# Indirect transfers that leave out empty slots, accumulating transfers that add the experts' results, and 32 unused bytes in SBUF

## The chip, the core and the metric

The program runs on one core of a Trainium2 chip: TensorE (PE) multiplies, VectorE (DVE) and ScalarE (ACT) work on tiles in SBUF and PSUM, GpSimd (POOL) does a little arithmetic and issues the indirect transfers, SyncE (SP) issues the other transfers, and 16 DMA engines carry all of them. The metric is the device time of one execution in microseconds. The kernel before took 2285.03 us (median of three runs, 2282.73 to 2285.18).

## The reference, cut to what matters

Two transformer blocks run over 256 tokens of width 1024, all in fp32. Most of the time goes into the mixture of experts of the first block's second layer: each token goes to its two best experts of eight, and an expert is a SwiGLU of width 3584.

```python
def moe_swiglu(xn, router, w_gu, w_down):
    logits = (xn @ router).astype(jnp.float32)
    top_v, top_i = lax.top_k(logits, TOP_K)              # TOP_K = 2 of N_EXPERTS = 8
    w = jax.nn.softmax(top_v, axis=-1)
    comb = jnp.sum(jax.nn.one_hot(top_i, N_EXPERTS, dtype=jnp.float32) * w[..., None], axis=-2)
    out = jnp.zeros_like(xn)
    for e in range(N_EXPERTS):
        out = out + comb[..., e:e + 1] * swiglu(xn, w_gu[e], w_down[e])
    return out
```

256 tokens times two choices over eight experts is 64 tokens for an expert on average.

## The kernel before

**Weights.** Every weight streams once from HBM. `fetch` (L473) loads 1 MB, four blocks of 128x512 fp32, into one of four `raw` buffers; ACT rounds it to `wh` (fp32r), DVE takes the rest `wl = raw - wh` (`split`, L395 and L396, 128x1024 at a time), and PE multiplies three times for each block: xh by wh, xl by wh, xh by wl. So 1 MB gives two `wh`, two `wl` and, in the experts, twelve matmuls of 512 columns. A `raw` buffer is free again, and SP can issue the next load, when DVE has made its second `wl`.

**Experts.** An expert has 128 slots, its tokens stand in the first of them, and the others are empty. For each expert (`expert`) there are seven blocks j: 48 matmuls with `moe_gu` weights, the activation (`ff_s`), and four transposes `tr<-cst,ff_s` that turn the result for the second product. Then come two halves n of the second product: 2 x 84 matmuls with `moe_down`. A branch serves experts with more than 128 tokens; the trace has no instruction of it.

**Rows in and out.** `mo_rows` in HBM holds the tokens' rows. For experts 1 to 7 `slots` (L1245) gathers 128 rows of 4 KB into `mo_got` by an indirect transfer with a list of row numbers `mo_ix`; an empty slot reads row 0. For experts 0 to 6 the result `mo_y` goes out by one indirect transfer for each half n (L1295) to `mo_res` in HBM: 512 rows for the tokens' first and second choice, and 128 spare rows for the empty slots, so that each slot writes a row of its own. `slot_tables` computes the row numbers on DVE with small operations on one to nine columns. Expert 7 goes another way: its result is brought back to the tokens by a matmul with `mo_PT` and added into `res` by DVE (L1305).

**Collecting.** During expert 7, at blocks j = 2 and 3, `collect` loads `mo_res` back (L1326, two transfers of 512 KB for each half n, on SP's queue between the weights), and POOL adds them into the residual tiles `res` (L1329, eight additions of 128x512).

**Order.** The instructions of each engine stand in one fixed order, which a scheduler made from the program; each engine runs its own list in order and waits on semaphores. A wait at the head of a list holds everything behind it. Tiles come from stocks (`sm`, `part`, `wp`) that lie behind the constant tiles (`keep`) in SBUF.

Of the kernel before, what the change touches and what calls it, by code (L numbers as in the profile page):

```python
# [7 lines left out]
F32 = mybir.dt.float32  # L8
F32R = mybir.dt.float32r
I32 = mybir.dt.int32  # L10
U32 = mybir.dt.uint32
AF = mybir.ActivationFunctionType
ALU = mybir.AluOpType
# [3 lines left out]
S = 256  # L17
D = 1024
NE = 8
# [4 lines left out]
TAPS_PE = 20  # L24
POOL_WINDOWS = (2, 4, 8, 16)
HQ = 64

# [65 lines left out]
def prep(i):  # L93

    f = {k: np.asarray(v) for k, v in i.items()}
    a = {}
# [6 lines left out]
    w = f["ev_w_in"][0].reshape(D, 4, 4, 128).transpose(0, 2, 1, 3).reshape(D, 2048)  # L103
# [13 lines left out]
    w = f["od_dw_w"][0][:TAPS_PE].reshape(TAPS_PE // 4, 4, 8, 4, 32).transpose(4, 2, 1, 0, 3)  # L117
# [12 lines left out]
    r = lambda s, n: list(range(s, s + n))  # L130
# [11 lines left out]
    w = f["w_o_2"].reshape(2, 5, 256, D)[:, [3, 4, 0, 1, 2]].reshape(2, 1280, D)  # L142
# [49 lines left out]
    w = Rows()  # L192
# [7 lines left out]
        w.add(f"lam{l}", f["diff_lambda_2"][l])  # L200
    a["rows"] = w.array().reshape(2, 1, -1)
    a["token"] = np.arange(S, dtype=np.float32).reshape(2, 128).T.copy()
    slot = 2 * S + np.arange(128, dtype=np.float32)
    a["spare"] = np.stack([slot, -slot], axis=1)
    a["bigrows"] = np.ascontiguousarray(np.stack([f["final_norm"], f["od_norm_moe"][0], f["od_pw2_b"][0]]))

    p = np.arange(128)
    t = np.arange(S)
    rc = []
    for win in POOL_WINDOWS:  # L210
        left = win // 2
        right = win - 1 - left
        n = np.minimum(t + right, S - 1) + 1 - np.maximum(t - left, 0)
# [90 lines left out]
class Build:  # L304
# [315 lines left out]
    def setup(self):  # L620
        nc, A = self.nc, self.A
        self.res = [self.keep(D, f"res{b}") for b in range(2)]
        cst = self.keep(384, "cst")
        ncol = A["cols"].shape[1]
        self.cols = self.keep(ncol, "cols")
        nc.scalar.dma_start(cst[:, :128], A["consts"][:, :128])
        nc.scalar.dma_start(self.cols[:, :8], A["cols"][:, :8])
        x = lambda n: [nc.sync.dma_start(self.res[b][:, n * 512:n * 512 + 512], A["x"][:, b, n * 512:n * 512 + 512]) for b in range(2)]
        x(0)
        self.ahead("w_in0", whole=False)  # L630
        x(1)
# [12 lines left out]
        self.warm(6)  # L644
        self.nrow = A["rows"].shape[2]
        self.rows, self.pre2, self.mem2 = {}, {}, {}
# [567 lines left out]
    def slot_tables(self, e):  # L1214

        nc = self.nc
        v = nc.vector
        P = self.picked  # L1220
        cws, rws, cw = self.slot_factors(e, P, self.moe_state[2])
        if e < NE - 1:
            to = self.sm(1, "mo_to")
            f = self.sm(NE + 1, "mo_to")
            v.tensor_copy(f, cw[:, NE + 2:])
            v.scalar_tensor_tensor(to, f[:, :1], self.spare[:, 1:2], f[:, 1 + e:2 + e], ALU.mult, ALU.add)
            back = self.sm(1, "mo_tx", I32)
            v.tensor_tensor(back, to, self.spare[:, 0:1], ALU.add)
        else:
            tr = self.scp(256)  # L1230
            for b in range(2):
                self.tp(tr[:, b * 128:b * 128 + 128], P[:, b])
            back = self.keep(S, "mo_PT", F32R)
            nc.scalar.copy(back, tr)
        return back, cws, rws, cw[:, NE + 1:NE + 2]

    def slots(self, e):


        nc = self.nc  # L1240
        back, cws, rws, at = self.slot_tables(e)
        ix = self.sm(1, "mo_ix", I32)
        nc.vector.tensor_copy(ix, at)
        got = self.sm(D, "mo_got")
        nc.gpsimd.indirect_dma_start(got, None, self.moe_state[1], bass.IndirectOffsetOnAxis(ap=ix.bitcast(U32), axis=0))  # L1245
        return got, back, cws, rws

    def turn(self, slots):
# [11 lines left out]
    def expert(self, e, rest, then=None):  # L1260

        nc = self.nc
        v = nc.vector
        gh, gl, back, cws, rws = self.turn(self.next_slots) if e else self.gathered
        xh = lambda k, b: gh[:, k]
        xl = lambda k, b: gl[:, k]
        hh = self.feat("mhh", F32R, 4, (8, 128))
        hl = self.feat("mhl", F32R, 4, (8, 128))
        base = e * D * 2 * DFE
        for j in range(7):  # L1270
            next(rest, None)
            pg, = self.ts(xh, xl, "moe_gu", base + 2 * j * D * 512, 8, nb=1)
            if e < NE - 1 and j == 2:
                self.pick(e + 1)
            if e < NE - 1 and j == 4:
                self.next_slots = self.slots(e + 1)
            if e == NE - 1 and j in (2, 3):
                self.collect(j - 2)
            pu, = self.ts(xh, xl, "moe_gu", base + (2 * j + 1) * D * 512, 8, nb=1)
            s = self.sm(512, "ff_s")  # L1280
            nc.scalar.activation(s, pg, AF.Silu, scale=rws)
            v.scalar_tensor_tensor(s, pu, rws, s, ALU.mult, ALU.mult)  # L1282
            tr = self.trp(4, 128)
            for k in range(4):
                self.tp(tr[:, k], s[:, k * 128:k * 128 + 128])
            self.split(hh[4 * j:4 * j + 4], hl[4 * j:4 * j + 4], tr)
        xh = lambda k, b: hh[k]
        xl = lambda k, b: hl[k]
        base = e * DFE * D
        for n in range(2):  # L1290
            py, = self.ts(xh, xl, "moe_down", base + n * DFE * 512, DFE // 128, nb=1)
            if not then:
                y = self.sm(512, "mo_y")
                nc.scalar.activation(y, py, AF.Copy, scale=cws)
                nc.gpsimd.indirect_dma_start(self.results[n], bass.IndirectOffsetOnAxis(ap=back.bitcast(U32), axis=0), y, None)  # L1295
                continue
            yh = self.sm(512, "mo_yh", F32R)
            yl = self.sm(512, "mo_yl", F32R)
            self.split_gain(yh, yl, py, cws)
            for b in range(2):  # L1300
                po = self.scp(512)
                self.mm(po, back[:, b * 128:b * 128 + 128], yh, True, False)
                self.mm(po, back[:, b * 128:b * 128 + 128], yl, False, True)
                r = self.res[b][:, n * 512:n * 512 + 512]
                v.tensor_tensor(r, po, r, ALU.add)  # L1305
            then.half(n)

    def clear_results(self):


        nc = self.nc
        zero = self.sm(512, "mo_zero")
        nc.gpsimd.memset(zero, 0.0)
        self.results = [self.dram.tile([2 * S + 128, 512], F32, name=f"mo_res{n}") for n in range(2)]
        for y in self.results:
            nc.scalar.dma_start(y[:2 * S].rearrange("(a p) d -> p a d", p=128), zero.unsqueeze(1).to_broadcast([128, 4, 512]))

        self.spare = self.keep(2, "mo_sp")
        nc.sync.dma_start(self.spare, self.A["spare"])

    def collect(self, n):

        nc = self.nc
        for w in range(2):
            z = self.sm((2, 512), "mo_z")
            nc.sync.dma_start(z, self.results[n][w * S:w * S + S].rearrange("(b p) d -> p b d", p=128))  # L1326
            for b in range(2):
                r = self.res[b][:, n * 512:n * 512 + 512]
                nc.gpsimd.tensor_tensor(r, r, z[:, b], ALU.add)  # L1329


    def angles(self):
# [767 lines left out]
```

## Time and profile before

| | us |
|---|---|
| median of three runs | 2285.03 |
| the profiled execution | 2284.27 |
| its span, first to last instruction | 2282.4 |
| PE busy | 2252.5 |
| DVE busy | 1798.6 |
| ACT busy | 1444.3 |
| POOL busy | 115.1 |

The profiled execution is 1.9 us longer than its span, and 0.76 us below the median of the runs. PE counts as busy in nearly all of the span, but its matmuls overlap and their ends are modelled, so how full PE really is has to be read from the time between matmuls in a stretch without a wait, not from the share. The granted clock was 0.999 of full on average.

### The profile page before, as it was taken

What the parts mean: (1) busy time and instruction counts of PE and PEld (TensorE: products, weight loads), DVE (VectorE), ACT (ScalarE), POOL (GpSimd) and SP (SyncE); (2) the same over time, 40 slices, a digit from 0 to 9 for tenths busy, and PEclk for the clock granted to TensorE, in tenths of its full rate; (3) what the DMA queues carried; (4) which work ended last, traced back from release to release, by engine and by line L of the source; (5) the groups of instructions that cost most, each with busy time, mean ns of one, the idle gap of its engine ahead of it and who ended that gap; (6) DMA issues with size and microseconds to landing.
All of it is one profiled execution on the core that took longest, in us unless ns stands there. A gap on an engine that the chain in (4) does not pass through costs nothing.

```text
span 2282.4 us, 34629 instructions
## 1 busy us (share of the span) xinstructions
PE 2252.5 (99%) x13069; PEld 1935.2 (85%) x13069; DVE 1798.6 (79%) x2601; ACT 1444.3 (63%) x2005; POOL 115.1 (5%) x163
## 2 busy tenths in 40 slices
PE   8999999999999999999999999989999999999999
PEld 8999998888878788888788878867788998888997
DVE  7656656986698898889898989888877885876883
ACT  5555545466567777777777777767765544665542
POOL 2100001301000000000000000020000000000000
PEclk9999999999999999999999999999999999999999
DMA  7544755954599989999999999989623555513553
GB/s 280 194 152 166 252 192 203 265 186 162 184 365 354 379 346 368 360 388 360 388 368 381 362 376 366 378 345 346 226 74 119 197 190 177 181 56 131 199 179 120
DMA packets 90891, 588.63 MB, mean 258 GB/s; under 512 B 11232, under 2 KB 12512, under 8 KB 24032
## 3 DMA queue, kind: packets, MB, share of 16 engines
q1 hardware_dynamic: 84752, 570.20, 67.7%
q0 software_dynamic: 4048, 12.97, 1.9%
q10 hardware_dynamic: 1920, 3.22, 0.4%
q8 instruction: 103, 1.69, 0.3%
q14 instruction: 68, 0.56, 0.1%
HBM read 577.31 MB, written 9.04 MB: 257 GB/s over the span
## 4 chain that ended last, share of the span: by engine, by line
PE 64%; DMA 4%; DVE 3%; ACT 1%; issue 1%; POOL 0%; ACTq 0%; DVEq 0%; POOLq 0%
PE acc L372 59%; DMA raw<-in_moe_gu_dram 3%; PE tr L376 3%; DVE wl L396 2%; PE sc L372 2%; ACT wh L395 1%; DMA raw<-in_moe_down_dram 0%; DMA ahead<-in_moe_gu_dram 0%; PE tr L372 0%; DVE res L556 0%; DVE xl L400 0%; POOL res L2043 0%; ACT at_p L1805 0%; DVE ff_s L1282 0%; DVE at_nm L1801 0%
## 5 line engine op out<-in xcount | busy, mean ns | idle before, releaser
L396 DVE TENSOR_TENSOR wl<-raw,wh 128x1024 fp32r<-128x1024 f32 x1054 | 1258.0, 1227 | 305.1 <-PE acc L372 176.9
L395 ACT CAST wh<-raw 128x1024 fp32r<-128x1024 f32 x1054 | 1060.1, 1047 | 431.5 <-PE acc L372 342.0
L372 PE MATMUL acc<-wh,mo_g 128*128 128x512 f32 x1568 | 488.8, 393 | 2.4 <-ACT wh L395 2.4
L372 PE MATMUL acc<-xl,wh 128*128 128x256 f32 x1440 | 399.1, 277 | 3.3 <-DVE xl L400 3.3
L372 PE MATMUL acc<-xh,wh 128*128 128x256 f32 x1440 | 399.7, 279 | 0.9 <-ACT xh L399 0.8
L372 PE MATMUL acc<-xh,wl 128*128 128x256 f32 x1440 | 398.0, 277 | 0.4 <-DVE wl L396 0.4
L372 PEld LDWEIGHTS acc<-wh,mo_g 128*128 128x128 f32 x1568 | 295.3, 189 | 64.8 <-ACT wh L395 3.5
L372 PE MATMUL acc<-wl,mo_g 128*128 128x512 f32 x784 | 314.8, 401 | 5.4 <-DVE wl L396 5.2
L372 PEld LDWEIGHTS acc<-xl,wh 128*128 128x128 f32 x1440 | 270.5, 188 | 5.2 <-DVE xl L400 4.5
L372 PEld LDWEIGHTS acc<-xh,wh 128*128 128x128 f32 x1440 | 270.0, 188 | 2.0 <-ACT xh L399 1.7
L372 PEld LDWEIGHTS acc<-xh,wl 128*128 128x128 f32 x1440 | 270.6, 188 | 0.6 <-DVE wl L396 0.6
L372 PEld LDWEIGHTS acc<-wl,mo_g 128*128 128x128 f32 x784 | 147.6, 188 | 49.4 <-DVE wl L396 21.4
L372 PE MATMUL acc<-wl,mhh 128*128 128x512 f32 x448 | 178.7, 399 | 2.4 <-DVE wl L396 1.6
L372 PE MATMUL acc<-wh,mhl 128*128 128x512 f32 x448 | 176.1, 393 | 0.0
L372 PE MATMUL acc<-wh,mhh 128*128 128x512 f32 x448 | 175.3, 391 | 0.0
L372 PEld LDWEIGHTS acc<-wl,mhh 128*128 128x128 f32 x448 | 84.2, 188 | 25.5 <-DVE wl L396 8.7
L372 PE MATMUL acc<-wl,hh 128*128 128x512 f32 x264 | 104.0, 394 | 0.0
L372 PE MATMUL acc<-wh,hl 128*128 128x512 f32 x264 | 103.5, 392 | 0.0
L372 PE MATMUL acc<-wh,hh 128*128 128x512 f32 x264 | 102.8, 390 | 0.0
L372 PEld LDWEIGHTS acc<-wh,mhl 128*128 128x128 f32 x448 | 84.1, 188 | 18.4
L372 PEld LDWEIGHTS acc<-wh,mhh 128*128 128x128 f32 x448 | 84.3, 188 | 17.2
L395 ACT CAST mhh<-tr 128x512 fp32r<-128x512 f32 x56 | 32.9, 588 | 94.8 <-PE tr L376 94.8
(439 smaller groups left out, 3103.8 us busy)
## 6 DMA issues: line engine op xcount, KB each, us to landing
raw<-in_moe_gu_dram SPq DMA_DIRECT2D x222, 1024.0 KB, 7.0
raw<-in_moe_down_dram SPq DMA_DIRECT2D x112, 1024.0 KB, 6.1
raw<-in_gu_dram SPq DMA_DIRECT2D x66, 1024.0 KB, 4.9
raw<-in_down_dram SPq DMA_DIRECT2D x30, 1024.0 KB, 4.8
raw<-in_w_in_b_dram SPq DMA_DIRECT2D x20, 1024.0 KB, 5.0
raw<-in_wkv_dram SPq DMA_DIRECT2D x16, 1024.0 KB, 5.0
raw<-in_pw_dram SPq DMA_DIRECT2D x12, 1024.0 KB, 4.8
raw<-in_wq_dram SPq DMA_DIRECT2D x8, 1024.0 KB, 4.8
```

What stands on the lines that cost most here:

```text
L372: self.nc.tensor.matmul(out, lhsT=l, rhs=r, start=start, stop=stop)
L376: self.nc.tensor.transpose(out, in_, self.ident[:n, :n])
L395: self.nc.scalar.copy(h, src)
L396: self.nc.vector.tensor_tensor(l, src, h.bitcast(F32), ALU.subtract)
```

## The change

Three edits. The indirect transfers get a bound: `bounds_check` with `oob_is_err=False` leaves out a row whose number lies past the bound. `slot_tables` now makes both lists of row numbers at once (`mo_tx`, two columns), and an empty slot gets 4096 (`PAST`), which is past either bound; so gathers for experts 1 to 6 read, and scatters for experts 0 to 6 write, the filled slots alone. For expert 7 the list is a plain copy, and an empty slot still reads row 0. The spare rows of `mo_res` and the small table `mo_sp` go.

`collect` becomes eight transfers on POOL's queue, each of which adds 128 rows of 2 KB from `mo_res` to a piece of `res` in SBUF (`accum_op`). They stand at block j = 0 of expert 7 for both halves, and the loads `mo_z` and POOL's eight additions go.

`self.keep(8, "shift")` takes 32 bytes of each partition behind `res`. `mo_sp`, which goes, took two numbers of the same pool.

```diff
     def setup(self):
         self.res = [self.keep(D, f"res{b}") for b in range(2)]
+        self.keep(8, "shift")
...
         cws, rws, cw = self.slot_factors(e, P, self.moe_state[2])
+        f = self.sm(NE + 2, "mo_f")
+        v.tensor_copy(f, cw[:, NE + 1:])
         if e < NE - 1:
-            to = self.sm(1, "mo_to")
-            f = self.sm(NE + 1, "mo_to")
-            v.tensor_copy(f, cw[:, NE + 2:])
-            v.scalar_tensor_tensor(to, f[:, :1], self.spare[:, 1:2], f[:, 1 + e:2 + e], ALU.mult, ALU.add)
-            back = self.sm(1, "mo_tx", I32)
-            v.tensor_tensor(back, to, self.spare[:, 0:1], ALU.add)
...
+            to = self.sm(2, "mo_to")
+            v.scalar_tensor_tensor(to, f[:, 1:2].to_broadcast([128, 2]), -PAST, f[:, 0:3 + e:2 + e], ALU.mult, ALU.add)
+            ix = self.sm(2, "mo_tx", I32)
+            v.tensor_scalar(ix, to, PAST, None, ALU.add)
+            return ix[:, 1:2], cws, rws, ix[:, 0:1]
...
-        ix = self.sm(1, "mo_ix", I32)
-        nc.vector.tensor_copy(ix, at)
         got = self.sm(D, "mo_got")
-        nc.gpsimd.indirect_dma_start(got, None, self.moe_state[1], bass.IndirectOffsetOnAxis(ap=ix.bitcast(U32), axis=0))
+        nc.gpsimd.indirect_dma_start(got, None, self.moe_state[1], bass.IndirectOffsetOnAxis(ap=ix.bitcast(U32), axis=0),
+                                     bounds_check=S - 1, oob_is_err=False)
...
-            if e == NE - 1 and j in (2, 3):
-                self.collect(j - 2)
+            if e == NE - 1 and j == 0:
+                self.collect()
...
-                nc.gpsimd.indirect_dma_start(self.results[n], bass.IndirectOffsetOnAxis(ap=back.bitcast(U32), axis=0), y, None)
+                nc.gpsimd.indirect_dma_start(self.results[n], bass.IndirectOffsetOnAxis(ap=back.bitcast(U32), axis=0), y, None,
+                                             bounds_check=2 * S - 1, oob_is_err=False)
...
-    def collect(self, n):
-
-        nc = self.nc
-        for w in range(2):
-            z = self.sm((2, 512), "mo_z")
-            nc.sync.dma_start(z, self.results[n][w * S:w * S + S].rearrange("(b p) d -> p b d", p=128))
-            for b in range(2):
-                r = self.res[b][:, n * 512:n * 512 + 512]
-                nc.gpsimd.tensor_tensor(r, r, z[:, b], ALU.add)
+    def collect(self):
+
+        for n in range(2):
+            for w in range(2):
+                for b in range(2):
+                    r = self.res[b][:, n * 512:n * 512 + 512]
+                    row = (2 * w + b) * 128
+                    self.nc.gpsimd.dma_start(r, self.results[n][row:row + 128], accum_op=ALU.add)
```

On POOL's list at the end of the experts, before (`mo_res_2946` is half 0 of the results, `mo_res_2947` half 1, `res_69` and `res_70` the residual's two pieces):

```order
L1245 DMA mo_got<-mo_rows,mo_ix 128x1024
L1295 DMA mo_res_2946<-mo_y,mo_tx 640x512
L1295 DMA mo_res_2947<-mo_y,mo_tx 640x512
L1329 TENSOR_TENSOR res_69<-res_69,mo_z 128x512
L1329 TENSOR_TENSOR res_70<-res_70,mo_z 128x512
```

There are eight such additions, four for each half. The same place now (`mo_res_2947` is half 0, `mo_res_2948` half 1):

```order
L1245 DMA mo_got<-mo_rows,mo_tx 128x1024
L1296 DMA mo_res_2947<-mo_y,mo_tx 512x512
L1327 DMA res_69<-mo_res_2947 128x512
L1327 DMA res_70<-mo_res_2947 128x512
L1327 DMA res_69<-mo_res_2947 128x512
L1327 DMA res_70<-mo_res_2947 128x512
L1296 DMA mo_res_2948<-mo_y,mo_tx 512x512
L1327 DMA res_69<-mo_res_2948 128x512
```

The four accumulating transfers of half 0 stand ahead of expert 6's last scatter, and those of half 1 behind it. On SP's list, before, the loads of the results stand among expert 7's weights:

```order
L473 DMA raw<-in_moe_gu_dram 128x2048 x11
L1326 DMA mo_z<-mo_res_2946 128x2x512 x2
L473 DMA raw<-in_moe_gu_dram 128x2048 x5
L1326 DMA mo_z<-mo_res_2947 128x2x512 x2
L473 DMA raw<-in_moe_gu_dram 128x2048 x12
```

Now nothing stands between them:

```order
L472 DMA raw<-in_moe_gu_dram 128x2048 x28
L472 DMA raw<-in_moe_down_dram 128x2048 x8
L2025 DMA brow<-in_bigrows_dram 128x1024
```

The lists of PE and ACT differ in a few places only, where a small group moved by a few instructions; DVE's has five instructions fewer.

## Rows read from the trace of the kernel before

**Rows 1.** The page, parts 1 and 2: engines, and DMA share in 40 slices.
```profile
PE 2252.5 (99%) x13069; PEld 1935.2 (85%) x13069; DVE 1798.6 (79%) x2601; ACT 1444.3 (63%) x2005; POOL 115.1 (5%) x163
DMA  7544755954599989999999999989623555513553
```

**Rows 2.** Stretches of the last experts (first row: columns).
```profile
core 0: us, PE busy (x) PEld busy (x) DVE busy (x) ACT busy (x) POOL busy (x), PEclk, DMA share, GB/s
1448.00:1488.00 40.00, 39.87 (x176) 32.19 (x175) 34.11 (x31) 30.53 (x34) 1.95 (x2) 1.00 1.00 398
1488.00:1528.00 40.00, 34.16 (x139) 25.25 (x139) 35.08 (x30) 26.14 (x30) 15.00 (x8) 0.96 0.88 339
```

**Rows 3.** The chain that ended last, 1483 to 1564 (start us, us, what).
```profile
1483.88 0.44 PE tr L376 x4
...
1493.66 9.43 DMA raw<-in_moe_gu_dram
...
1503.60 2.32 DVE wl L396
...
1551.11 0.44 PE tr L376 x4
1551.54 11.07 PE acc L372 x48
1562.61 0.44 PE tr L376 x4
```

**Rows 4.** DVE in order of time, 1494 to 1525 (start us, us, what).
```profile
1497.41 4.03 DVE L396 TENSOR_TENSOR wl<-raw,wh 128x1024 fp32r<-128x1024 f32 x2 [0.25 <-ACT wh L395]
1501.77 6.41 DVE L396 TENSOR_TENSOR wl<-raw,wh 128x1024 fp32r<-128x1024 f32 x4 [0.33 <-ACT wh L395]
...
1508.77 2.35 DVE L396 TENSOR_TENSOR wl<-raw,wh 128x1024 fp32r<-128x1024 f32 x2
...
1514.78 4.23 DVE L396 TENSOR_TENSOR wl<-raw,wh 128x1024 fp32r<-128x1024 f32 x2 [0.71 <-ACT wh L395]
```

**Rows 5.** POOL in order of time, 1440 to 1530.
```profile
1451.62 0.98 POOL L1295 DMA_INDIRECT mo_res<-mo_y,mo_tx  x1 [100.21 <-ACT mo_y L1294]
1470.89 0.97 POOL L1295 DMA_INDIRECT mo_res<-mo_y,mo_tx  x1 [18.28 <-ACT mo_y L1294]
1496.83 8.00 POOL L1329 TENSOR_TENSOR res<-res,mo_z 128x512 f32<-128x512 f32 x4 [24.97 <-DMA mo_z<-mo_res]
1514.39 7.00 POOL L1329 TENSOR_TENSOR res<-res,mo_z 128x512 f32<-128x512 f32 x4 [9.56 <-DMA mo_z<-mo_res]
```

**Rows 6.** Transfers issued 1486 to 1520 (xcount, KB each, median us to landing).
```profile
raw<-in_moe_gu_dram SPq DMA_DIRECT2D x10, 1024.0 KB, 9.0
mo_z<-mo_res SPq DMA_DIRECT2D x4, 512.0 KB, 8.4
```

**Rows 7.** POOL's queue of transfers, whole span (packets, MB, share of 16 engines).
```profile
q0 software_dynamic: 4048, 12.97, 1.9%
```

**Rows 8.** The same queue, 620 to 1610, and its issues.
```profile
q0 software_dynamic: 2128, 7.34, 1.9%
...
mo_res<-mo_y,mo_tx POOLq DMA_INDIRECT x14, 6.9
mo_got<-mo_rows,mo_ix POOLq DMA_INDIRECT x7, 9.9
```

**Rows 9.** POOL in order of time, 720 to 760.
```profile
725.33 1.02 POOL L1295 DMA_INDIRECT mo_res<-mo_y,mo_tx  x1 [58.08 <-ACT mo_y L1294]
744.59 0.97 POOL L1295 DMA_INDIRECT mo_res<-mo_y,mo_tx  x1 [18.24 <-ACT mo_y L1294]
745.87 1.49 POOL L1245 DMA_INDIRECT mo_got<-mo_rows,mo_ix  x1 [0.30 <-issue]
```

**Rows 10.** The chain, 745 to 1160.
```profile
749.94 9.97 DMA raw<-in_moe_gu_dram
```

**Rows 11.** Tile res, 1480 to 1640 (ns min/median/max, first and last start).
```profile
L1305 DVE TENSOR_TENSOR res<-sc,res x4: 680/686/693, 1582.8 to 1607.5; 128x512 f32<-128x512 f32 x4
```

**Rows 12.** Tiles mo_ix and mo_sp.
```profile
L1243 DVE CAST mo_ix<-sc x7: 152/154/158, 663.0 to 689.6; 128x1 int32<-128x1 f32 x7
L1319 SPq DMA_DIRECT2D mo_sp<-in_spare_dram x1: 425/425/425, 38.8 to 38.8; - x1
```

**Rows 13.** What PE waited for, 1610 to the end (us, times, longest).
```profile
PE tr L376 <- DVE at_o L1845: 1.2, 2, 0.7
```

More of the change, by code (lines that the diff above doesn't have):

```diff
@@ L26 @@
 HQ = 64
+PAST = 4096.0
 def _inv_freq(rot):
@@ L202, in prep @@
     a["token"] = np.arange(S, dtype=np.float32).reshape(2, 128).T.copy()
-    slot = 2 * S + np.arange(128, dtype=np.float32)
-    a["spare"] = np.stack([slot, -slot], axis=1)
     a["bigrows"] = np.ascontiguousarray(np.stack([f["final_norm"], f["od_norm_moe"][0], f["od_pw2_b"][0]]))
@@ L1221, in slot_tables @@
         cws, rws, cw = self.slot_factors(e, P, self.moe_state[2])
+        f = self.sm(NE + 2, "mo_f")
+        v.tensor_copy(f, cw[:, NE + 1:])
         if e < NE - 1:
-            to = self.sm(1, "mo_to")
-            f = self.sm(NE + 1, "mo_to")
-            v.tensor_copy(f, cw[:, NE + 2:])
-            v.scalar_tensor_tensor(to, f[:, :1], self.spare[:, 1:2], f[:, 1 + e:2 + e], ALU.mult, ALU.add)
-            back = self.sm(1, "mo_tx", I32)
-            v.tensor_tensor(back, to, self.spare[:, 0:1], ALU.add)
-        else:
-            tr = self.scp(256)
-            for b in range(2):
[L1232 to L1235, printed above, removed]
+            to = self.sm(2, "mo_to")
[3 more added lines that the diff above has]
+            return ix[:, 1:2], cws, rws, ix[:, 0:1]
+        tr = self.scp(256)
+        for b in range(2):
+            self.tp(tr[:, b * 128:b * 128 + 128], P[:, b])
+        back = self.keep(S, "mo_PT", F32R)
+        nc.scalar.copy(back, tr)
+        ix = self.sm(1, "mo_tx", I32)
+        v.tensor_copy(ix, f[:, 0:1])
+        return back, cws, rws, ix
     def slots(self, e):
         nc = self.nc
-        back, cws, rws, at = self.slot_tables(e)
-        ix = self.sm(1, "mo_ix", I32)
-        nc.vector.tensor_copy(ix, at)
+        back, cws, rws, ix = self.slot_tables(e)
         got = self.sm(D, "mo_got")
-        nc.gpsimd.indirect_dma_start(got, None, self.moe_state[1], bass.IndirectOffsetOnAxis(ap=ix.bitcast(U32), axis=0))
+        nc.gpsimd.indirect_dma_start(got, None, self.moe_state[1], bass.IndirectOffsetOnAxis(ap=ix.bitcast(U32), axis=0),
+                                     bounds_check=S - 1, oob_is_err=False)
         return got, back, cws, rws
@@ L1313, in clear_results @@
         nc.gpsimd.memset(zero, 0.0)
-        self.results = [self.dram.tile([2 * S + 128, 512], F32, name=f"mo_res{n}") for n in range(2)]
+        self.results = [self.dram.tile([2 * S, 512], F32, name=f"mo_res{n}") for n in range(2)]
         for y in self.results:
-            nc.scalar.dma_start(y[:2 * S].rearrange("(a p) d -> p a d", p=128), zero.unsqueeze(1).to_broadcast([128, 4, 512]))
-        self.spare = self.keep(2, "mo_sp")
-        nc.sync.dma_start(self.spare, self.A["spare"])
-    def collect(self, n):
-        nc = self.nc
-        for w in range(2):
-            z = self.sm((2, 512), "mo_z")
-            nc.sync.dma_start(z, self.results[n][w * S:w * S + S].rearrange("(b p) d -> p b d", p=128))
-            for b in range(2):
-                r = self.res[b][:, n * 512:n * 512 + 512]
-                nc.gpsimd.tensor_tensor(r, r, z[:, b], ALU.add)
+            nc.scalar.dma_start(y.rearrange("(a p) d -> p a d", p=128), zero.unsqueeze(1).to_broadcast([128, 4, 512]))
+    def collect(self):
+        for n in range(2):
+            for w in range(2):
+                for b in range(2):
+                    r = self.res[b][:, n * 512:n * 512 + 512]
+                    row = (2 * w + b) * 128
+                    self.nc.gpsimd.dma_start(r, self.results[n][row:row + 128], accum_op=ALU.add)
     def angles(self):
```

## The prediction, written before the changed kernel ran

> **What bounds the kernel now.** I read the engines' busy times first: PE is busy for 2252.5 us of the span, and the DMA engines are at nine tenths through the slices of the experts and near half elsewhere [rows 1]. A share alone does not say which of the two sets the end, so I went to the chain that ended last. Between two waits it is a regular beat: 48 matmuls in 11.07 us and four transposes in 0.44, so that one group of transposes follows the last by 11.50 us (1551.11 to 1562.61) [rows 3]. That is PE at its own pace, 0.23 us for a matmul of 512 columns. A block of that length uses 16 weight tiles of 128x512 fp32, 4.19 MB, which asks for 365 GB/s. Then I cut the last experts into stretches: from 1448 to 1488 the DMA engines had no idle share at all and moved 398 GB/s [rows 2]. So in the experts PE is the bound and DMA stands some 8% behind it: whatever holds PE is paid in full, and transfers that are added or left out count as far as they exceed this margin.
>
> [...]
>
> **The change part by part.** *The additions on POOL and the loads mo_z go.* From the transposes at 1483.88 to those at 1562.61 there are six beats (expert 7's blocks 1 to 6): 78.73 us where six undisturbed ones take 6 x 11.50 = 69.0 [rows 3]. The stretch loses 9.7 us. DVE's own excess is 1.68 + 1.71 + 1.88 = 5.3 us [rows 4]; the rest is what stands in order behind it, the loads of mo_z beside the weights (median landing 9.0 us here, and one of 9.43 on the chain [rows 3, 6]), and the lower clock of the stretch. All of it hangs on these additions and loads, and both leave the place: -9.7 us. What is late next there is PE itself.
>
> *Eight accumulating transfers come.* They move what mo_z moved, 2.1 MB, but on POOL's queue and earlier: the order puts the first four right behind expert 6's scatter of half 0, issued at 1451.62, and the last four behind that of half 1 at 1470.89 [rows 5]. Each group waits for the scatter to land (median 6.9 us [rows 8]), and in a group the third transfer adds to the same bytes as the first and waits for it. With 8.4 us for a landing as mo_z had [rows 6], the groups run from about 1459 to 1475 and 1478 to 1495: 36 us, most of them in the stretch where DMA is already full. Behind the waits on POOL stands only the scatter of half 1, and for `res` nobody asks before DVE's addition at 1582.8 [rows 11]; even with landings of twice that length the last is down by 1540, so the wait itself costs nothing. What costs is DMA time. No row shows a transfer that adds. Low end: it is a copy, at the price of POOL's queue in the experts, 1.9% of 990 us for 7.34 MB [rows 8], 2.56 us per MB, so 5.4 us. High end: every byte goes twice, as the old value has to be read too: 10.7 us. The dearest copies of that queue lie between: its 1.9% of 2282.4 us for 12.97 MB [rows 7] leave 24.6 us for the 5.63 MB outside the experts, 4.4 us per MB, or 9.2 us for these. I take 8, between the ends. The margin of 8% gives back 3 us in 36. PE loses 5.0 us, with ends of 2.4 and 7.7.
>
> *Empty slots' rows are left out.* With 64 filled slots of 128 on average, half of what scatters and gathers move goes: of 1.05 MB or 2.7 us of DMA time in an expert, 1.3. How much of that is PE's? The scatters of half 0 at 725.33 and 1451.62 lie six experts apart, 121.05 us each [rows 5, 9]. PE's own pace gives seven beats of 11.50, 168 matmuls of 0.2306 and eight transposes in 0.88: 120.1. So an expert loses 0.95 us to everything together, 5.7 us in six experts, and no more can come back. Some of it does hang on these transfers: behind the scatter and the gather at 744.59 and 745.87 [rows 9] a weight load on the chain takes 9.97 us [rows 10]. Half the traffic, half of the loss, would be 2.8 us; I take 1.5, because the filled slots are the first of the list and not spread over it. Ends 0 and 5.7 us.
>
> [...]
>
> *Small edits.* Seven casts of about 0.15 us leave DVE, all between 663 and 690 [rows 12], where PE was at work on the chain; the 1 KB load of mo_sp leaves SP at 38.8; SP's four issues of mo_z go, from a queue that mostly waits for a free buffer. I cost them at nothing; without that cover they are worth 1 us together. The 32 bytes take the place that mo_sp gave up, so the stocks lie where they lay, and only some constant tiles move by 32 bytes: nothing. As mo_z takes four buffers fewer from its stock, later tiles fall into other buffers and can meet other waits; behind the experts PE's longest wait of any kind is 0.7 us in a group of 1.2 [rows 13], so I allow 1.5 us either way and none in the sum.
>
> Sum: -9.7 + 5.0 - 1.5 = -6.2 us on the profiled execution's 2284.27 gives 2278.1; this execution is 0.76 us below the median of the runs, so 2278.8. The ends of the terms give -13.0 to -2.0, and with that offset 2272.0 to 2283.0.
>
> **Rivals.** *The add is paid twice and nothing comes of the empty slots.* DMA time 10.7 us, PE loses 7.7, the skipped rows give 0: -2.0 us, 2283.0, no change that can be measured. For it: the old value must be read from somewhere, and the transfers run where DMA has no idle share [rows 2]; against it, that they ask HBM for no more than mo_z did, and a read in SBUF need not take the engine a second full time. [...]
>
> *The accumulating transfers starve the weights.* If an engine handles an adding row much more slowly than a copied one, say four times, 21.4 us of DMA time fall into 36 us in which the weights want all of it. PE then loses 18.4 us: -9.7 + 18.4 - 1.5 = +7.2, 2292.0, slower. It decides from 14.2 us of DMA time on (11.2 gained plus the margin of 3), which is 2.6 times a copy. [...] Against it: the dearest copies on that queue come to 9.2 us.
>
> *The bound doesn't spare the engines.* If a row left out still passes as a packet, the last term is 0: -4.7 us, 2280.3, on the edge of what can be told. For it only that no row shows such a transfer.
>
> **How the numbers follow.** The forecast has 0.58, the add paid twice 0.22, starvation 0.13, the bound without effect 0.07. The measurement of this kernel can tell about 0.2%, 4.6 us, so faster means under 2280.5 and slower above 2289.6. From the forecast 0.53 falls under 2280.5 and 0.05 into no change; the third rival is split evenly. Faster 0.56, no change 0.30, slower 0.14 (starvation, and 0.01 for an ill turn of later buffers). The forecast's own range is 2272 to 2283. The range for 8 in 10 reaches down to 2270, for a better turn behind the experts, and up to 2289, part of the way to starvation.
>
> **What would show it.** After the change: DVE's weight tiles at 1.22 us all through expert 7, POOL about 15 us less busy, the six beats of expert 7 back at 11.50 us from block 3 on, and no lower clock before 1530. If the 5.0 us are right, PE pauses in the experts' last change, 1460 to 1500, and the weights land later than 7 us there. The skipped rows show as fewer bytes on POOL's queue (3.3 to 3.7 MB less in the experts beside what the adds bring) and experts of about 120.8 us instead of 121.05. The prediction is wrong if PE still loses its beat in blocks 2 and 3, if the accumulating transfers' landings run past 1582 and DVE's addition waits, or if the experts' period does not move and the pauses at 1460 to 1500 exceed 10 us.

## The result, and the profile after

The changed kernel takes 2296.24 us (median of 5 runs, 2295.67 to 2299.15) where the kernel before, timed beside it, takes 2285.18: the ratio is 1.0052, with an interval of 1.0038 to 1.0066. It is 11 us slower. I had forecast 2278.8.

The profiled execution took 2295.67 us, its span is 2293.9. To see where the time went I compared the starts of the same matmul (both kernels issue 13069, in nearly the same order) in the two traces. Up to matmul 3200, at 439 us, the changed kernel falls 8.16 us behind. It keeps that through the router (8.13 at matmul 4800). In the experts it gains 6.6 us (1.5 behind at matmul 9200). Behind them it loses another 10.05. So there are two results, a gain in the experts and a larger loss in stages that the change seems not to touch.

**The experts.** POOL in order of time, 1440 to 1540, after the change, answers to [rows 5]. The eight additions are gone, eight accumulating transfers stand in their place:

```profile
1457.21 1.10 POOL L1296 DMA_INDIRECT mo_res<-mo_y,mo_tx  x1 [98.16 <-ACT mo_y L1295]
1464.60 1.94 POOL L1327 DMA_DIRECT2D res<-mo_res  x2 [6.29 <-DMA mo_res<-mo_y,mo_tx]
1473.91 0.85 POOL L1327 DMA_DIRECT2D res<-mo_res  x1 [7.38 <-DMA res<-mo_res]
1477.77 0.88 POOL L1327 DMA_DIRECT2D res<-mo_res  x1 [3.01 <-DMA res<-mo_res]
1478.95 1.07 POOL L1296 DMA_INDIRECT mo_res<-mo_y,mo_tx  x1 [0.31 <-ACT wh L394]
1489.05 1.77 POOL L1327 DMA_DIRECT2D res<-mo_res  x2 [9.03 <-DMA mo_res<-mo_y,mo_tx]
1497.51 0.85 POOL L1327 DMA_DIRECT2D res<-mo_res  x1 [6.69 <-DMA res<-mo_res]
1501.29 0.87 POOL L1327 DMA_DIRECT2D res<-mo_res  x1 [2.93 <-DMA res<-mo_res]
```

DVE's weight tiles in the same stretch take 2.36 us for two, where [rows 4] had 4.03 and 4.23:

```profile
1498.07 2.36 DVE L395 TENSOR_TENSOR wl<-raw,wh 128x1024 fp32r<-128x1024 f32 x2 [0.59 <-ACT wh L394]
1514.58 2.36 DVE L395 TENSOR_TENSOR wl<-raw,wh 128x1024 fp32r<-128x1024 f32 x2 [0.31 <-ACT wh L394]
```

The same two stretches as in [rows 2] (columns as there): PE's pause has moved from the second to the first and become smaller, and the clock no longer falls.

```profile
1448.00:1488.00 40.00, 38.02 (x159) 29.03 (x159) 31.05 (x28) 27.31 (x29) 5.83 (x6) 1.00 1.01 362
1488.00:1528.00 40.00, 38.80 (x170) 29.80 (x169) 34.57 (x34) 30.89 (x34) 3.49 (x4) 1.00 1.03 387
```

And the chain, 1483 to 1570, which answers to [rows 3]:

```profile
1478.05 10.11 DMA raw<-in_moe_gu_dram
...
1492.94 0.44 PE tr L375 x4
...
1500.46 10.29 DMA raw<-in_moe_gu_dram
...
1518.27 0.44 PE tr L375 x4
1518.71 11.06 PE acc L371 x48
1529.77 0.44 PE tr L375 x4
...
1564.27 0.44 PE tr L375 x4
```

From 1492.94 to 1564.27 the six beats take 71.33 us instead of 78.73. The last four take 11.50 each, the first two 25.33 together: PE waits there for a weight load of 10.29 us, beside the second group of accumulating transfers. Ahead of the six beats, from the scatter of half 0 to the first of these transposes, PE needs 1492.94 - 1457.21 = 35.73 us, before 1483.88 - 1451.62 = 32.26.

**The loss.** Its place is found with the page's list of instructions. Three groups are dearer, and they are all the matmuls of 256 columns. Before (line engine operation, count, busy us, mean ns), and after:

```profile
L372 PE MATMUL acc<-xl,wh 128*128 128x256 f32 x1440 | 399.1, 277 | 3.3 <-DVE xl L400 3.3
L372 PE MATMUL acc<-xh,wh 128*128 128x256 f32 x1440 | 399.7, 279 | 0.9 <-ACT xh L399 0.8
L372 PE MATMUL acc<-xh,wl 128*128 128x256 f32 x1440 | 398.0, 277 | 0.4 <-DVE wl L396 0.4
```

```profile
L371 PE MATMUL acc<-xl,wh 128*128 128x256 f32 x1440 | 404.8, 281 | 3.4 <-DVE xl L399 3.4
L371 PE MATMUL acc<-xh,wh 128*128 128x256 f32 x1440 | 405.4, 283 | 1.2 <-ACT xh L398 0.8
L371 PE MATMUL acc<-xh,wl 128*128 128x256 f32 x1440 | 403.9, 281 | 0.5 <-DVE wl L395 0.5
```

A matmul overlaps the next (277 ns for one here, 113.3 from start to start below), so these durations aren't steps. The step, from start to start, is read from the chain where it holds nothing but such matmuls. From 1800 on, before and then after:

```profile
1799.95 40.12 PE acc L372 x354
```

```profile
1799.95 40.16 PE acc L371 x341
```

40.12 us for 354 is 113.3 ns for one, 40.16 for 341 is 117.8. PE waits for nothing in either, it is busy for all of the time, and the granted clock of these stages is 1.00 in both. There are two steps, one 4.5 ns longer than the other, and PE keeps to one through a stream of some 957 matmuls. Where does it change? The chain from 1760 to 1790, before and then after (`sc` are the multiplications by `ones` which spread a norm over the partitions, line 1974 and following):

```profile
1766.60 5.46 PE acc L372 x48
1772.06 0.45 PE sc L372 x4
1772.51 17.59 PE acc L372 x155
```

```profile
1768.14 5.46 PE acc L371 x48
1773.59 0.44 PE sc L371 x4
1774.04 16.02 PE acc L371 x136
```

Ahead of `sc` both have 113.8 ns, behind it the kernel before has 113.5 and the changed one 117.8. Of the 8.16 us lost up to matmul 3200, 7.12 are steps from one matmul of 256 columns to the next, and of the 10.05 behind matmul 9200, 8.28 (1.83 more are steps of 512 columns in the last stage, 233 ns instead of 229). The operands of these matmuls lie at the same bytes in both kernels in the first stages, which already show both steps. What moved is `ones`, `cst` and the other constants, by the 32 bytes that I had costed at nothing.

The step changes at other small groups too, where `ones` takes no part. Before, ahead of the multiplications at 204 us, there are transposes between two stretches (22 steps lie between the first two lines, 18 between the last two):

```profile
195.30 0.28 PE L372 MATMUL acc<-xl,wh 128*128 128x256 f32 x1
...
197.89 0.28 PE L372 MATMUL acc<-xh,wl 128*128 128x256 f32 x1
198.01 0.60 PE L376 MATMUL tr<-cst,res 128*128 128x128 f32 x4
...
199.03 0.28 PE L372 MATMUL acc<-xh,wl 128*128 128x256 f32 x1
...
201.07 0.28 PE L372 MATMUL acc<-xh,wl 128*128 128x256 f32 x1
```

That is 117.7 ns ahead of the transposes and 113.3 behind them. And behind the first `sc` by `ones`, at 23 us, the step is 113.5 ns before and 113.4 in the changed kernel. So `ones` is not all that sets the step; most of the loss arises in the three long streams behind its multiplications at 204, 1772 and 2109 us.

### The profile page after: what moved, and what is told of

It reads as the page before. It is cut to its first block, busy times and chain, and to the rows that moved or that the text cites. A ratio compares the mean times of both kernels' runs of the same rounds, so it can differ in the third digit from the quotient of the medians.

```text
span 2293.9 us, 34636 instructions
## 1 busy us (share of the span) xinstructions
PE 2268.4 (99%) x13069; PEld 1949.5 (85%) x13069; DVE 1792.5 (78%) x2596; ACT 1447.1 (63%) x2005; POOL 107.2 (5%) x163
## 4 chain that ended last, share of the span: by engine, by line
PE 65%; DMA 3%; DVE 2%; ACT 1%; issue 1%; POOL 0%; ACTq 0%; DVEq 0%; POOLq 0%
PE acc L371 60%; PE tr L375 3%; DMA raw<-in_moe_gu_dram 2%; PE sc L371 2%; DVE wl L395 2%; ACT wh L394 1%; DMA raw<-in_moe_down_dram 1%; DMA ahead<-in_moe_gu_dram 0%; PE tr L371 0%; DVE res L555 0%; DVE xl L399 0%; POOL res L2041 0%; ACT at_p L1803 0%; DVE ff_s L1283 0%; DVE at_o L1843 0%
## 5 line engine op out<-in xcount | busy, mean ns | idle before, releaser
L371 PE MATMUL acc<-xl,wh 128*128 128x256 f32 x1440 | 404.8, 281 | 3.4 <-DVE xl L399 3.4
L371 PE MATMUL acc<-xh,wh 128*128 128x256 f32 x1440 | 405.4, 283 | 1.2 <-ACT xh L398 0.8
L371 PE MATMUL acc<-xh,wl 128*128 128x256 f32 x1440 | 403.9, 281 | 0.5 <-DVE wl L395 0.5
```

The source lines that it names most:

```text
L371: self.nc.tensor.matmul(out, lhsT=l, rhs=r, start=start, stop=stop)
```

## The experiments

A place is given here modulo 64 bytes: before, the constants `cst` and `ones` lie at 0, and the stocks of activations and weights at 32. The changed kernel has all at 32. The stretch of the chain in the table holds nothing but matmuls of 256 columns: some 354 of them in 40 us are the short step, 341 the long one.

| run | `ones` | activations | weights | us | ratio to before (interval) | from 1800 | from 2150 |
|---|---|---|---|---|---|---|---|
| before (timed beside each) | 0 | 32 | 32 | 2285 | 1 | 354 | 354 |
| the change | 32 | 32 | 32 | 2296.24 | 1.0052 (1.0038 to 1.0066) | 341 | 340 |
| pad_old_place | 0 | 32 | 32 | 2282.24 | 0.9989 (0.9980 to 0.9997) | 354 | 354 |
| before_sp_front | 32 | 32 | 32 | 2299.90 | 1.0069 (1.0056 to 1.0082) | 340 | 341 |
| no_pad | 0 | 0 | 0 | 2298.91 | 1.0067 (1.0054 to 1.0080) | 341 | 341 |
| both_pads | 32 | 0 | 0 | 2285.48 | 0.9998 (0.9990 to 1.0007) | 354 | 354 |
| pad64 | 0 | 32 | 32 | 2281.57 | 0.9985 (0.9977 to 0.9994) | 354 | 354 |
| pad_before_ones | 32 | 32 | 32 | 2295.81 | 1.0050 (1.0036 to 1.0064) | 341 | 354 |
| ones_only | 32 | 32 | 32 | 2299.88 | 1.0057 (1.0038 to 1.0076) | 353 | 354 |
| cst_only | 0 | 32 | 32 | 2284.70 | 0.9996 (0.9987 to 1.0006) | 354 | 354 |
| after_dg | 32 | 32 | 32 | 2296.74 | 1.0050 (1.0032 to 1.0069) | 341 | 341 |
| old_place_dg | 0 | 32 | 32 | 2280.91 | 0.9973 (0.9962 to 0.9984) | | |
| after_w | 32 | 32 | 0 | 2319.84 | 1.0144 (1.0121 to 1.0167) | 338 | 342 |
| old_place_w | 0 | 32 | 0 | 2313.40 | 1.0116 (1.0099 to 1.0133) | 341 | 342 |

**Is it the 32 bytes?** Theory 1: the place of the constants sets the step. Its rivals: the changed order of instructions sets it, or chance. Two runs part them, one with the change and the constants where they were, one without the change and the constants moved.

pad_old_place:

```diff
 setup, behind self.res
-        self.keep(8, "shift")
 clear_results, at its end (where mo_sp was taken)
+        self.keep(8, "shift")
```

> The changed kernel, with the 32 unused bytes not in front of the constant tiles but behind them, where the removed tile mo_sp lay: every constant tile and every stock lies at the byte where it lay in the kernel before; everything else of the change stays. Theory 1: the place of the constant tiles decides in which of two steps (113 or 118 ns) a matmul of 256 columns follows the last, and that alone made the changed kernel slow. Then the step is 113.9 ns on average as before in the stages ahead of 440 us and behind 1760 us, the gain of the experts (6.6 us in the traces) stays, and the time is 2277 to 2280 us. Theory 2: the other order of instructions or the missing load of mo_sp sets the step. Then nothing changes against the changed kernel: 2295 to 2299 us and a step of 117 ns. Theory 3: the step falls by chance from run to run: single times spread over both.

before_sp_front, an edit of the kernel before:

```diff
 setup, behind self.res
+        self.spare = self.keep(2, "mo_sp")
 clear_results
-        self.spare = self.keep(2, "mo_sp")
```

> The kernel before, with one edit: the tile mo_sp (32 bytes) is taken right behind the residual tiles instead of behind the constants, so that the constant tiles lie 32 bytes further on, as in the changed kernel; all stocks stay where they are, and no instruction is added, removed or moved. Theory 1 (the place of the constant tiles sets the step): the matmuls of 256 columns go from 113.9 to about 117 ns, 4300 of them at 3.2 ns more and what was faster elsewhere, so 2285 + 11 to 18 = 2296 to 2303 us, slower by 0.5 to 0.8%. Theory 2 (order of instructions): no difference, 2283 to 2287 us.

Theory 1 holds in both. With the bytes in the old place the changed kernel falls from 2296.24 to 2282.24 us, 2 us above the range that I had expected. The kernel before, with the place of one tile changed and no instruction touched, rises to 2299.90. Its chain around 1774 has the same turn at `sc` as the changed kernel's, from 113.8 ns to 25.44 / 216 = 117.8:

```profile
1768.75 5.46 PE acc L372 x48
1774.20 0.44 PE sc L372 x4
1774.65 25.44 PE acc L372 x216
```

The order of instructions is ruled out as the cause, and so is chance from run to run: the five runs of before_sp_front (2296.44 to 2302.60) and the eleven of pad_old_place (2279.70 to 2285.18) don't touch.

**By what rule?**

no_pad (all that lies behind the constants comes 32 bytes earlier):

```diff
-        self.keep(8, "shift")
```

> The changed kernel without the 32 unused bytes at all: the constant tiles lie as in the kernel before, but all that comes behind them, the stocks of activations and weights included, lies 32 bytes earlier. If only the constants' place counts (theory 1a): 2277 to 2280 us, as with the bytes in the old place. If the place of the stocks, or of constants against stocks, counts as well (theory 1b): the steps of 256 columns change in all stages, in a direction that nothing yet tells; 2270 to 2300 us. Theory 2 (order of instructions): 2295 to 2299 us.

both_pads (the 32 bytes in front, and 32 more at the end of the constants):

```diff
 clear_results, at its end
+        self.keep(8, "shift2")
```

> The changed kernel with 32 unused bytes in front of the constant tiles and 32 more behind them: constants 32 bytes and stocks 32 bytes further on than in the kernel before. Byte addresses modulo 64 so far: constants 0 and stocks 32 gave 2282 us, both 32 gave 2296, both 0 gave 2299. Here constants 32, stocks 0. If the difference of the two decides (theory 1c): fast, 2280 to 2285 us, step of 256 columns near 114 ns behind 1760 us. If the constants have to lie at 0 and the stocks at 32, each by itself (theory 1d): 2293 to 2300 us.

pad64 (as both_pads, with 64 bytes in front):

```diff
-        self.keep(8, "shift")
+        self.keep(16, "shift")
```

> The changed kernel with 64 unused bytes in front of the constant tiles and 32 behind them: constants and stocks both 64 bytes further on than in the kernel before, so that every address modulo 64 is as before. If the place modulo 64 decides: as with the bytes in the old place, 2280 to 2285 us. If any move of the constants away from where they lay is slow (another period, or a place of its own): 2293 to 2300 us.

Constants where they were and stocks moved is slow (no_pad), both moved by 32 is fast in its steps (both_pads), and 64 bytes change nothing (pad64). So theory 1c holds for the four combinations: in the long streams, constants and stocks at the same place modulo 64 give the long step, at different ones the short. The traces part as sharply: from matmul 9200 to the end the change, before_sp_front, no_pad and after_dg lose 9.98 to 10.14 us against before, pad_old_place, both_pads, pad64 and cst_only between -0.18 and 0.23. both_pads has the short step in all long streams and yet 2285.48 us. Its profile shows a stretch of lower clock (0.91 from 360 to 400), and its profiled execution is the fastest of eleven; what costs the other ones 4 us against pad64 is open.

**Which constant?**

pad_before_ones (`cst` stays):

```diff
-        self.keep(8, "shift")
         cst = self.keep(384, "cst")
...
+        self.keep(8, "shift")
         self.ones = self.keep(128, "ones")
```

> The changed kernel with the 32 unused bytes behind the tiles cst (identity for transposes) and cols and in front of ones: the identity lies as in the kernel before, ones and the tiles behind it 32 bytes further on, as in the changed kernel. If the tile ones sets the step (its matmuls stand where the step flips in the trace): 2294 to 2299 us as with all constants moved. If the identity sets it (transposes stand at the flips too): 2277 to 2280 us. If both do: between, 2283 to 2292 us. Theory 2 (order of instructions): 2295 to 2299 us.

ones_only and cst_only, made from pad_old_place:

```diff
-        self.ones = self.keep(128, "ones")
+        self.ones = self.keep(144, "ones")[:, 8:136]
```

```diff
-        cst = self.keep(384, "cst")
+        cst = self.keep(400, "cst")[:, 8:392]
```

> The changed kernel with the 32 unused bytes in the old place and the tile ones alone moved by 32 bytes (what lies behind it is 64 further on, so modulo 64 as before). If the multiplications by ones, which spread the norms over the partitions, set the step of the matmuls behind them: 2293 to 2300 us, step near 117 ns. If the identity cst or another constant sets it: 2280 to 2285 us.

> The same with the tile cst alone (the identity for transposes) moved by 32 bytes. If ones sets the step: 2280 to 2285 us. If the identity does, too: 2290 us or more, step of 115 ns or more.

By the times it is `ones`: alone moved it makes 2299.88, `cst` alone moved 2284.70. But pad_before_ones and ones_only spread much more than the others (2288.35 to 2300.83 and 2290.39 to 2303.02). Their profiled executions are the fastest of theirs, and show the long step in some stages and the short in others: in ones_only it averages 116.5 ns from 200 to 440 us, and 113.4 behind 1750. So these traces don't show the long step in every long stream, and the steps of the slower executions are not known. With only a part of the constants moved the long step is likely, not certain.

**Which partner of `ones`?**

after_dg (from the changed kernel) and old_place_dg (from pad_old_place):

```diff
-            dg = k.sm(128, "nt_dg")
+            dg = k.sm(136, "nt_dg")[:, 8:136]
```

> The changed kernel as it is (ones at 32 modulo 64), with the diagonal tiles nt_dg alone, which ones multiplies to spread the norms, read 32 bytes further on in their buffers (at 0 modulo 64). If it is the pair of places of ones and nt_dg that sets the step behind it: unequal now, 2280 to 2286 us, step near 114 ns. If ones counts against the stocks of activations and weights that the later matmuls read, or by its own place: still 2293 to 2300 us.

> The fast variant with the 32 bytes in the old place (ones at 0 modulo 64), with nt_dg moved in the same way, to 0 modulo 64. If the pair sets the step: equal now, 2293 to 2300 us, 117 ns behind the spreading of the norms at 204, 388, 1772 and 2109 us. If ones counts against the other stocks or by its own place: 2280 to 2285 us.

after_w and old_place_w, likewise:

```diff
 setup, ahead of self.res
+        self.wp.tile([128, 8], F32, name="w_pad", tag="w_pad", bufs=1)
```

> The changed kernel as it is (ones and the stocks of activations at 32 modulo 64), with the stocks of weights (raw, wh, wl) alone moved by 32 bytes, to 0 modulo 64. If ones counts against the weights: unequal now, 2280 to 2286 us, step near 114 ns. If ones counts against the activations: equal still, 2293 to 2300 us. If activations against weights count by themselves, as in the pieces put ahead (119.8 ns where equal, 116.7 where not): every stage with 256 columns changes, and this variant and the next alike.

> The fast variant with the 32 bytes in the old place (ones at 0, activations at 32 modulo 64), with the weights' stocks moved in the same way, to 0. If ones counts against the weights: equal now, 2293 to 2300 us. If against the activations: 2280 to 2285 us, step near 114 ns. If activations against weights count by themselves: as the variant before.

`nt_dg` is not the partner: the slow kernel stays slow, the fast one fast. (The profiled execution of old_place_dg took 5810 us where its ten others took 2277.53 to 2282.32; why is open, and no step is taken from its trace.) The weights' runs answer another question than I asked. With activations and weights at different places modulo 64, both kernels become slower by far, 34.0 and 27.5 us over before. The step averages 118.1 and 117.5 ns, so it is long wherever `ones` lies (in after_w it is 118.7 from 1800 and 117.3 from 2150), and an expert takes 122.4 and 122.2 us. So activations against weights count by themselves, and whether `ones` counts against the one or the other stays open.

**The step by itself.** probe puts ahead of the kernel before 16 blocks of two multiplications by ones, a copy and 48 matmuls of 256 columns; probe2 has 16 runs of 48 in the order of the real stages, without a pause. The places are changed between blocks.

```diff
+        for s in (0, 8, 0, 8):
+            x = [t[:, s:s + 256] for t in xs]
+            for p, q in ((0, 0), (8, 8), (0, 8), (8, 0)):
...
+                    self.mm(o, a[:, p:p + 128], r, True, True)
...
+                    self.mm(o[:, 0], h, x[0], i == 0, False)
+                    self.mm(o[:, 0], h, x[1], False, False)
+                    self.mm(o[:, 0], l, x[0], False, i == 15)
```

> The kernel before with a piece put ahead of it that only loads PE: 16 blocks, each of two multiplications of a 128x128 tile of ones by a 128x128 tile (as in the spreading of the norms), a copy of the result to SBUF, and 48 matmuls of 256 columns that read it. Between the blocks change the places modulo 64 bytes of the ones and of the tile that they multiply, and of the copy that the matmuls read (32 in the first and third four blocks, 0 in the others). If the pair of the places of these two tiles sets the step by itself: blocks with equal places (the first two of each four) at 117 to 118 ns, with unequal ones (the last two) at 113. If the step depends on something of the place in the kernel that this piece doesn't have (transposes between, weights arriving, waits of other lengths): one step in all blocks, or steps without regard to the places. In the whole some 130 us more than before, of no meaning.

> The kernel before with another piece ahead of it: 16 runs of 48 matmuls of 256 columns in the order of the real stages, and ahead of each, without a wait, two multiplications by ones, as at 204 us of the kernel before, where PE doesn't pause either. In each four: ones and its partner at 32 and 32, 0 and 32, 0 and 0, 32 and 0 modulo 64; the tiles that the 48 matmuls move at 32 in the first and third four and at 0 in the others. If the pair of places sets the step of a stream that doesn't pause: 117 to 118 ns in the first and third run of a four, 113 to 114 in the second and fourth. If the places of the tiles that the 48 matmuls read themselves set it, as in the first piece (119.8 and 116.7 ns): all four alike, and the fours different. The time in the whole has no meaning.

In both the pair of the places of ones and its partner changes nothing. The place of the moved tiles does: 119.6 to 120.0 ns a step with moved tiles and weights both at 32, 116.6 to 116.8 with the moved tiles at 0 (one block 117.8). Neither piece shows the 113.3 of the kernel, which has moved tiles and weights at 32 too. That isolates an effect of the places on matmuls alone, but not the one that decides here.

**The parts of the change.** accum_only is the kernel before with the new `collect` (called at block 0 of expert 7), and nothing else of the change; bound_only is pad_old_place with the old `collect` put back, the reverse of this edit:

```diff
-            if e == NE - 1 and j in (2, 3):
-                self.collect(j - 2)
+            if e == NE - 1 and j == 0:
+                self.collect()
```

> The kernel before with one part of the change: the eight accumulating transfers in place of POOL's additions and the mo_z loads. Scatters and gathers still move the empty slots' rows, and every tile lies where it lay. My terms -9.7 and +5.0: 4.7 us less from the start of expert 6's last blocks to the end of expert 7, and in the whole 2280 to 2282 us. If an addition costs twice a copy: 2 us less, 2283. If most of the gain of the experts comes from the rows left out: no difference, 2284 to 2286.

> The changed kernel with POOL's additions and the mo_z loads put back and the 32 bytes in the old place: what is left of the change is the rows of empty slots, left out by scatters and gathers, and the edits of the index tables. My term -1.5: a period of an expert of 120.8 us instead of 121.05 and in the whole 2283 to 2285 us, not to be told from before. If the rows left out are worth the larger part of the gain: 2280 to 2281 us, and a period of 120.3. If nothing: 121.05 us and 2285.

accum_only takes 2283.57 us, ratio 0.9987 (0.9978 to 0.9996), which is nearer to the 2283 that I had named for an addition at twice a copy than to my 2280 to 2282; bound_only 2283.49, ratio 0.9995 (0.9983 to 1.0006), not to be told from before. By the traces: the six beats of expert 7 take 71.3 us in the changed kernel, 71.7 in accum_only and 71.3 in pad_old_place; 78.7 before, 79.4 in bound_only and 76.8 in before_sp_front. So accumulating instead of adding on POOL gives the gain there. The way from expert 6's last scatters to these beats is 3.5 us longer with the accumulating transfers (28.1 to 29.4 us from the same matmul in ten kernels with them and with the weights in place, 24.4 to 25.1 in the three without).

POOL's queue, 620 to 1610 (packets, MB, share of 16 engines), in bound_only, in accum_only and in the changed kernel:

```profile
q0 software_dynamic: 2128, 4.05, 1.1%
```

```profile
q0 software_dynamic: 3280, 9.44, 3.0%
```

```profile
q0 software_dynamic: 3280, 6.15, 2.3%
...
res<-mo_res POOLq DMA_DIRECT2D x8, 256.0 KB, 9.1
...
mo_res<-mo_y,mo_tx POOLq DMA_INDIRECT x14, 6.9
```

Against [rows 8] the empty slots' rows are 7.34 - 4.05 = 3.29 MB and 0.8% of 990 us, 7.9 us of DMA time. The packets stay 2128: a row left out still counts as a packet, without its bytes. The accumulating transfers are 1.1 to 1.2%, 10.9 to 11.9 us for 2.1 MB. That their rows are shorter is not the reason: in the changed kernel's trace an added row of 2 KB takes 176 ns in its packet, a copied packet of 4 KB on the same queue 168, and the six copied packets of 2 KB 85.

## Why the prediction was wrong, step by step

- **The bound.** Right where the runs tested it: what PE lost in matmul steps came out in the time in full. I had taken the width of a beat as PE's own fixed pace, though, and in the stages of 256 columns it is not fixed (113.3 or 117.8 ns).
- **"The additions on POOL and the loads mo_z go": -9.7.** The mechanism is right. Before, PE's pause from 1488 (139 matmuls in 40 us at a clock of 0.96, 176 in the 40 before [rows 2]) lay beside POOL's additions [rows 5] and DVE's tiles of 4.03 and 4.23 us for two [rows 4]. Now these tiles are at 1.18 us each, the clock stays at 1.00, and the beats are 11.50 us from block 3 on. What is gained is 78.73 - 71.33 = 7.4, since 2.3 us of the six beats now go to the transfers that came; the next term has them. The size rested on one profile, though: before_sp_front, with the same additions and loads, loses 7.8 us there (76.8 against 69.0).
- **"Eight accumulating transfers come": +5.0.** They cost 3.5 us ahead of the six beats and 2.3 in them, 5.8, inside the ends. Their DMA time, 10.9 to 11.9 us, is that of the first rival (10.7, every byte twice) and not the 8 that I took. By [rows 8] a copy of these bytes would be 5.4 us, so an adding transfer took 2.0 to 2.2 times a copy; by what mechanism is not shown. PE lost 5.8 and not the 7.7 that I worked out for that price, so by this sum my margin of 3 us was too small. (In the rival of starvation 2285.0 and 7.2 make 2292.2, not 2292.0; nothing hangs on it.) They landed later than I thought, the last after 1501, and nobody asked for `res` before DVE at 1584.4, as said.

```profile
L1307 DVE TENSOR_TENSOR res<-sc,res x4: 681/686/692, 1584.4 to 1609.0; 128x512 f32<-128x512 f32 x4
```

- **"Empty slots' rows are left out": -1.5.** The bytes are right (3.29 MB; I said 3.3 to 3.7). I had brought 2.8 us down to 1.5 for the place of the filled slots in the list; no run shows that this place counts. The experts' period is 120.63 us in the changed kernel and 120.57 in bound_only, against 121.05, so 2.5 to 2.9 us in six experts. But before_sp_front, which moves all rows, has 120.59, and pad64 and cst_only, which leave the empty ones out, have 120.97 and 121.03. The term can't be told from nothing.
- **Small edits, later buffers: nothing.** Right as far as seen: behind matmul 9200 pad_old_place differs from before by 0.02 us.
- **"Only some constant tiles move by 32 bytes: nothing."** This is the step that failed: I put the move at nothing and gave no reason. By before_sp_front it costs 14.5 us (ratio 1.0069), by pad_old_place against the change 14.0. No rival had it either. No row I had read spoke of places in SBUF, but the profile showed the two steps: the page's means are averages over them, and before, from 72 to 85 us, the step is 117.8 ns.

The sum without that step was -6.2. In the traces the experts (matmul 4800 to 9200) give 6.6 in the changed kernel and 6.9 in pad_old_place. That this lies so near the sum is in part luck: seven more traces with the whole change and the weights in place gain between 2.6 (cst_only) and 7.7 us (both_pads) there, and before_sp_front, in which no instruction changed, gains 4.3. In the time the fast variants gain less: 0.9973 to 0.9998 in the five with the whole change that are not slow, so 0.5 to 6 us, around 2.5. In pad_old_place's trace 3.2 us of the gain go in one place ahead of the experts, where the clock falls. That kernel and then before, 600 to 612 (columns as in [rows 2]):

```profile
600.00:606.00 6.00, 6.00 (x36) 5.29 (x36) 3.21 (x22) 1.09 (x2) 0.00 (x0) 0.89 0.48 194
606.00:612.00 6.00, 6.00 (x19) 4.95 (x18) 2.44 (x10) 1.05 (x1) 0.00 (x0) 0.54 0.40 149
```

```profile
600.00:606.00 6.00, 6.00 (x41) 5.20 (x40) 3.88 (x22) 1.54 (x2) 0.00 (x0) 1.00 0.38 153
606.00:612.00 6.00, 6.00 (x36) 5.24 (x35) 4.42 (x17) 2.19 (x5) 0.00 (x0) 1.00 0.53 179
```

From 606 to 612 the granted clock is 0.54, though PE had been busy without a pause (6.00 of 6.00 us), and 19 matmuls get done where the kernel before has 36. Seven of the fifteen traces that I compared show such a stretch between 600 and 640 us (0.73 to 0.95 on average over 10 us), with fast and with slow steps alike, the profiles of before and of the change not. Why there is open, and no run tests it.

The versions that beat both kernels are pad_old_place and pad64, with ratios of 0.9989 and 0.9985 (and old_place_dg with 0.9973): the change with `ones` left at a place modulo 64 other than that of the stocks. accum_only, the accumulating transfers by themselves with every tile in its place, comes as far with 0.9987.

## What to carry to other kernels

Before an edit that moves tiles is costed at nothing, list what moves in SBUF and by how much: in a kernel that PE bounds, 32 bytes were worth more (14.0 us) than the whole rest of the change (0.5 to 6). Read PE's own pace as matmuls per stretch in stages without waits, before and after. Here a step that differed there, at the same granted clock, was no matter of queues or of order, and two edits that moved the places alone showed it. The accumulating transfers cost the DMA engines about twice a copy here (10.9 to 11.9 us where a copy would be 5.4), and paid because they took work off POOL beside which DVE's weight tiles came late for PE (4.03 and 4.23 us for two, 2.36 without it).

## What the hardware showed that I had not expected

- Matmuls of 256 columns have two steps, 113.3 and 117.8 ns at a granted clock of 1.00, and keep to one through streams of some 957. The step turns at other small groups too, transposes among them (from 117.7 to 113.3 ns at 198 us of the kernel before). In the three long streams behind multiplications by `ones` it went with the place of that tile, which the streams don't read, modulo 64 bytes against the stocks: with the weights in place, short in seven traces with different places, long in four with equal ones, and mixed in pad_before_ones and ones_only. With the weights alone moved, in after_w and old_place_w, the step averages 118.1 and 117.5 ns, and from 1800 on old_place_w has 341 matmuls where pad_old_place has 354, so the place of one operand against another counts too. By which mechanism places count is not shown.
- Activations and weights at different places modulo 64 (after_w, old_place_w) make the whole 27 to 34 us longer than before, though the pieces put ahead, with tiles of other stocks, were faster so (116.7 against 119.8 ns). No single rule found here covers both.
- A row that an indirect transfer's bound leaves out keeps its packet (2128 in before and in bound_only) and loses its bytes, and 3.29 MB less were 7.9 us less of DMA time.
